# Side work between weight products: transposes emitted a step or two behind what makes their inputs

## The chip, the core and the metric

The kernel runs on one core of one Trainium2 chip. The metric is the device time of one launch in microseconds (us). The engines named below are PE (the matrix engine), DVE (the vector engine), ACT (the scalar engine), POOL (GpSimd) and SP (which starts most transfers). A transpose is a product on PE against the identity matrix; its result lands in PSUM and is copied out by DVE or ACT.

## What is computed

A step of a two-layer decoder trunk: 2048 new prompt tokens, and 8 sequences that each add 4 tokens to a state that is already there (the "sample"). Width 1024, fp32 throughout. Each layer, cut to what matters:

```
z = rms(x) @ w_in                       # aq, ak, av, ag, dqkv, dg, db, da
q = rope(rms(aq)); k = rope(rms(ak))    # 8 query heads, 2 key heads, 64 wide
att = sink_attend(q, k, av, window=128) * silu(ag)
q, k, v = split(silu(conv4(dqkv)))      # 4 heads, 128 wide
beta = sigmoid(db); g = -exp(a_log) * softplus(da + dt_bias)
dn = gated_delta(l2n(q), l2n(k), v, beta, g, state)
y = x + concat(att, rms(dn) * silu(dg)) @ w_out
```

The sample's rows go through the same layer with cached keys and values and a delta state of their own. The outputs are both rows, and the windows and states of each layer.

## The kernel before

The program goes through the two layers, and in each through four groups of 512 tokens. A group's input is held transposed, as a high and a low part in a rounded fp32 format, and a product with a block of weights takes three passes (high by high, high by low, low by high; `block`, L465). The weights come as a stream of pieces: SP fetches a piece, ACT rounds it (L248), POOL takes the rest (L249, `lo = raw - hi`). A group's blocks take some 68 pieces: keys, values and gates 0 to 3, the delta rule's keys 4 to 11, queries of the attention 12 to 19, the delta rule's queries 20 to 27 and values 28 to 35, two blocks of gates 36 to 51, and the output product 52 to 67.

All other work stands beside these products. It is written as generators, each with its `yield`s, and an object `Tasks` emits it between the pieces: `add(gen, n, s, e)` says that the generator has n steps, spread evenly over the pieces s to e, and `step()` runs, after each piece, as many as are due (the numbers stand in a table `W`). The order of emission is not yet the order on an engine: the framework's scheduler takes the emitted instructions, with their dependences, and sets for each engine its own order. On the engine itself instructions then run in that order, each waiting for its inputs.

The generators that the change touches:

- `k_task` normalises and rotates the group's keys (`head_norm_rope`, L370 to L384, on the tile `kall`), then transposes them, four transposes into one PSUM tile (L567), and copies them out as high and low (L571 to L573). It has one step, at piece 4.
- `q_task` does the same for the queries, in two halves of four heads each (`qh`), a step for each half, then for each of four tiles of tokens four transposes (L625) and copies (L629, L630).
- `att_task`, per tile of tokens: scores of a query tile with the keys (L647, L648, in two steps), exponentials, the division by their sum (L677, eight DVE instructions on the tile `Pt`), transposes of the softmax rows (L682), and the product with the values.
- `sample_att`: for the sample the softmax rows `Ps` are scaled (L1089) and transposed (L1094).
- `sample_head`: the delta rule of one head of the sample; its gated row (L426) is transposed in the last step (L1296). Within it also a product with the states (L1286).

Around them stand `gate_task` (the delta rule's gates: L397 to L410, copies into a tile `gx`, L585, then running sums as three products, L587, L597, L598) and `conv_tile`, the short convolution on DVE (L703 to L705) which empties the PSUM tiles of products. PSUM has four tiles for products (`mm`) and four for all else (`px`).

The step of the task list, which turns windows into emission:

```python
want = n if self.at >= e else n * (self.at - s) // (e - s)
while x[4] < want:
    next(gen, None)
    x[4] += 1
```

Of the kernel before, what the change touches and what calls it, by code (L numbers as in the profile page):

```python
# [24 lines left out]
TS = NB_S * LS  # L25
# [5 lines left out]
T = 512  # L31
# [6 lines left out]
# the blocks after the first one: (transposed, index), of k, k, aq, q, q, v, v, dg, ag, ag; where each lies in zs  # L38
# [4 lines left out]
# columns of the first constant array  # L43
C_ID, C_U, C_BAND = 0, 128, 256
C_END = 512
# windows of pieces in which the work beside the products with weights is emitted; see group()
W = dict(k1=4, pre0=13, pre1=19, q0=17, q1=31, inv0=20, inv1=41, invv=-3, att0=23, att1=46, qk0=36, qk1=38, sc0=44, sc1=52, sa0=-4, sa1=17, sp0=7, sp1=26, sh0=60, shd=8, shl=10, wla=4, wraw=4, xn0=2, xn1=8, sla=3, md0=53, md1=55, ma0=45)

# columns of the second one (sample): the rows are there three times
# [5 lines left out]
def _constants():  # L55
    i = np.arange(P)
    c = np.zeros((P, C_END), np.float32)
# [38 lines left out]
    # of kS and qS: row (4 b's, 32) -> tokens, k three times, q  # L96
# [17 lines left out]
class Tasks:  # L114
    """Work emitted between the pieces of the products with weights: each generator over a window of pieces."""
# [24 lines left out]
def hybrid_kernel(ctx, tc, a):  # L140
# [52 lines left out]
    def rsqrt(out, x):  # L193
        """x ** -0.5 of positive x: a guess from the exponent, three of Newton's steps"""
# [9 lines left out]
    def silu2(out, z, n, m):  # L204
        """2 silu(z), z in PSUM or SBUF"""
        th = f2([P, m], name="th")
        A.activation(th[:n], z, AF.Tanh, scale=0.5)  # L207
        V.scalar_tensor_tensor(out, th[:n], 1.0, z, op0=ALU.add, op1=ALU.mult)  # L208

    # keys of each group of heads, transposed, twice, as hi; then both groups' lo  # L210
# [25 lines left out]
    def fetch(first=False):  # L236
        """asks for the next pieces of the weights, as (hi, lo) of float32r, and whole"""
# [14 lines left out]
    def getw():  # L252
        """the next piece; later ones are under way"""
        fetch()
        return wready.pop(0)
# [43 lines left out]
    def x_norm(L, gi, out, first=False):  # L299
        """the group's input, transposed, [128, 2 k, T] each, and the factors of its norm on all partitions"""  # L300
# [31 lines left out]
    def x_scale(L, kh, x, out):  # L332
        """half of the normed input: [128, (hi lo), 4 k, T]"""
# [10 lines left out]
    def sx_stage(L, out):  # L344
        """the sample's normed input, transposed: [128, 8 k, TS]"""
# [18 lines left out]
    def head_norm_rope(x, n, gain, cos, sin):  # L364
        """RMS norm and rotation of x [n, a, b, 64] in place; cos, sin [n, a, 16]"""
# [20 lines left out]
    def gates(L, ba, n, c):  # L386
        """2 beta and log decay g of ba [n, c, 8] as [n, c, 4]"""
# [26 lines left out]
    def delta_out(po, rq, rq2, gate, on, n):  # L414
        """gated RMS norm of o = rq * po [n, m, 128]; the gain and a factor 0.5 are left out"""
# [12 lines left out]
    def qscale(ss, n, m):  # L428
        """the factors of q's norm from its sums of squares: r / sqrt(128), and that squared / 128"""
# [7 lines left out]
    def kscale(ss, b2, n, m):  # L437
        """beta / (2 |k|^2), and 0.5 sqrt of k's sums of squares"""
# [9 lines left out]
    def block(X, n, kpp, feat, consume, sg=None, every=1):  # L448
        """all tokens' columns of the next block of weights (or their transposes), k by k; X(k) gives the tokens'
        transposed rows [128, (hi lo), T]; sg, the sample's products, run ahead"""  # L450
# [23 lines left out]
    class SampleProducts:  # L474
        """the sample's products with the weights, a piece at a time, four tiles of the array at once: each k of the
        piece, parts of its columns; blocks are (columns, k per piece, consumer)"""
# [933 lines left out]
```

## Time and profile before

| | |
|---|---|
| median of 3 runs | 2594.18 us (2593.74 to 2595.14) |
| span of the profiled execution | 2594.2 us |
| PE busy | 2443.9 us, 94% of the span, 14580 instructions |
| DVE busy | 1844.2 us, 71% |
| ACT busy | 1183.7 us, 46% |
| POOL busy | 993.1 us, 38% |

The page lists busy time for each engine, then the span in slices, transfers, the chain of work that ended last, and the costliest groups of instructions. From the same execution a trace can be asked for the waits of an engine (who waited for whom, and how long), for a timeline of single instructions with the idle time before each, and for the busy time and the granted clock of PE in a stretch. Numbers such as L567 are lines of the kernel before. In the kernel with the change the same statement stands a few lines lower: L567 becomes L569, L585 and L587 become L587 and L589, L597 and L598 become L599 and L600, L625 and L630 become L628 and L633, L647 and L648 become L650 and L651, L682 becomes L687, L703 to L705 become L708 to L710, L1296 becomes L1303. L370 to L410 and L465 stay.

### The profile page before, as it was taken

The page shows a single profiled execution, that of the slowest core. Times are in us where ns is not written, and L with a number is a line of the kernel's source. Part 1 is how long each engine was busy: PE and PEld are TensorE (multiplying, and loading weights), DVE is VectorE, ACT ScalarE, POOL GpSimd, SP SyncE. Part 2 cuts the span into 40 slices and gives each one's busy share as a digit, 9 for nine tenths or more (in the row PEclk, how much of TensorE's full clock was granted, in tenths as well). Part 3 has the DMA queues.
Part 4 walks back from the last instruction along what each step waited for, and adds up shares of the span by engine and source line. Part 5 has one row for each costly group of instructions (what it writes and reads, how often), then busy time and mean ns, then how long its engine had stood idle before and what let it go on. Part 6 is the DMA issues. An engine that isn't in the chain of part 4 may idle for free. (4 is left out here: it accounts for less than half of the span.)

```text
span 2594.2 us, 43148 instructions
## 1 busy us (share of the span) xinstructions
PE 2443.9 (94%) x14580; PEld 1874.0 (72%) x14580; DVE 1844.2 (71%) x5509; ACT 1183.7 (46%) x3244; POOL 993.1 (38%) x1148
## 2 busy tenths in 40 slices
PE   6999999999999999999999999999998999999999
PEld 5766787668776677767876678776787667777677
DVE  6576777767788765776766757888577885767764
ACT  4444544445353444544534445444543444445442
POOL 2352353423424324353343523444243352344423
PEclk9988999889998999989999999999999999999999
DMA  3212342113432124211332113421233312232113
GB/s 125 83 58 60 112 144 80 49 48 106 143 102 67 52 74 147 92 49 54 108 121 81 54 50 129 135 83 42 84 119 115 101 55 84 83 125 82 52 46 110
DMA packets 185970, 227.30 MB, mean 88 GB/s; under 512 B 58524, under 2 KB 92932, under 8 KB 185684
## 3 DMA queue, kind: packets, MB, share of 16 engines
q1 hardware_dynamic: 185748, 224.54, 27.1%
q8 instruction: 115, 1.88, 0.3%
q14 instruction: 107, 0.88, 0.1%
HBM read 197.30 MB, written 30.19 MB: 88 GB/s over the span
## 5 line engine op out<-in xcount | busy, mean ns | idle before, releaser
L249 POOL TENSOR_TENSOR lo<-raw,hi 128x512 fp32r<-128x512 f32 (+1 forms) x576 | 748.4, 1304 | 1499.4 <-ACT hi L248 1469.4
L465 PE MATMUL mm<-xT,hi 128*128 128x512 f32 x2048 | 699.1, 412 | 4.7 <-ACT hi L248 3.6
L248 ACT CAST hi<-raw 128x512 fp32r<-128x512 f32 (+1 forms) x576 | 341.2, 595 | 604.6 <-PE mm L465 431.8
L465 PE MATMUL mm<-hi,xT 128*128 128x512 f32 (+1 forms) x1536 | 466.4, 377 | 4.7 <-DVE halo L705 2.9
L465 PEld LDWEIGHTS mm<-xT,hi 128*128 128x128 f32 x2048 | 399.6, 196 | 96.7 <-issue 7.7
L465 PE MATMUL mm<-xT,lo 128*128 128x512 f32 x1024 | 420.8, 411 | 0.4 <-POOL lo L249 0.3
L465 PEld LDWEIGHTS mm<-hi,xT 128*128 128x128 f32 x1536 | 280.5, 195 | 58.9 <-issue 14.3
L465 PE MATMUL mm<-lo,xT 128*128 128x512 f32 (+1 forms) x768 | 283.3, 369 | 0.0
L465 PEld LDWEIGHTS mm<-xT,lo 128*128 128x128 f32 x1024 | 201.7, 197 | 41.5 <-issue 1.9
L465 PE MATMUL mm<-mixA,hi 128*128 128x512 f32 x512 | 168.9, 398 | 0.0
L465 PE MATMUL mm<-mixD,hi 128*128 128x512 f32 x512 | 165.0, 394 | 0.0
L465 PEld LDWEIGHTS mm<-lo,xT 128*128 128x128 f32 x768 | 149.6, 195 | 18.4 <-issue 0.6
L652 DVE CUSTOM_DVE_ANT_0 Pt<-px,cst 128x256 f32<-128x256 f32 (+1 forms) x256 | 94.7, 413 | 95.3 <-PE px L648 94.5
L703 DVE SCALAR_TENSOR_TENSOR KQ<-mm,pc,KQ 128x511 f32<-128x511 f32 (+2 forms) x192 | 141.6, 738 | 23.9 <-ACT KQ L700 23.6
L666 ACT ACTIVATE Pt<-Pt,nm 128x256 f32<-128x256 f32 (+1 forms) x256 | 125.2, 491 | 8.2 <-DVE nm L658 8.2
L682 PE MATMUL px<-cst,Pt 128*128 128x128 f32 x496 | 92.9, 295 | 26.8 <-DVE Pt L677 24.2
L677 DVE TENSOR_SCALAR Pt<-Pt,rd 128x256 f32<-128x256 f32 (+1 forms) x256 | 116.4, 506 | 1.1
L772 POOL TENSOR_TENSOR Xh<-Xh,pr 128x126 f32<-128x126 f32 (+22 forms) x248 | 106.9, 431 | 18.1
L647 PE MATMUL px<-kT,q 128*128 128x256 f32 (+1 forms) x256 | 102.7, 401 | 11.4 <-ACT th L207 9.3
L465 PEld LDWEIGHTS mm<-mixD,hi 128*128 128x128 f32 x512 | 95.9, 188 | 23.1 <-issue 2.4
L770 POOL TENSOR_TENSOR pr<-At,Xh 128x126 f32<-128x126 f32 (+22 forms) x248 | 93.7, 378 | 48.0 <-DVE vT L208 16.1
L465 PEld LDWEIGHTS mm<-mixA,hi 128*128 128x128 f32 x512 | 96.4, 189 | 21.0 <-issue 2.0
(397 smaller groups left out, 4426.0 us busy)
## 6 DMA issues: line engine op xcount, KB each, us to landing
raw<-in_wf_dram SPq DMA_DIRECT2D x256, 256.0 KB
raw<-in_wt_dram SPq DMA_DIRECT2D x128, 256.0 KB
raw<-in_w_out_dram SPq DMA_DIRECT2D x128, 256.0 KB
raw<-in_w_dram SPq DMA_DIRECT2D x64, 132.0 KB
x<-in_x_prompt_dram SPq DMA_DIRECT2D x16, 512.0 KB
xr<-in_x_prompt_dram SPq DMA_DIRECT2D x32, 256.0 KB
y<-xr SPq DMA_DIRECT2D x32, 256.0 KB
x<-y SPq DMA_DIRECT2D x16, 512.0 KB
```

What stands on the lines that cost most here:

```text
L248: A.copy(hi, raw)
L249: G.tensor_sub(lo, raw, hi.bitcast(F32))
L465: PE.matmul(pss[u], lhs, rhs, start=(k == 0 and q == 0), stop=(k == 7 and q == 2))
L647: PE.matmul(sps[kv][:, jj, c0:], q, kT[:, kv, cols], start=True, stop=False)
L652: V.tensor_tensor_reduce(out=Pt[kv][:, j, c0:], in0=sps[kv][:, jj, c0:], in1=band[:, c0:], scale=1.0, scalar=NEG, op0=ALU.add, op1=ALU.max ...
L666: A.activation(Pt[kv][:, j, c0:], Pt[kv][:, j, c0:], AF.Exp, bias=nm[:, h:h + 1], scale=0.125, accum_out=den[:, h:h + 1])
L677: V.tensor_scalar(Pt[kv][:, j, c0:], Pt[kv][:, j, c0:], rd[:, h:h + 1], None, op0=ALU.mult)
L682: PE.transpose(pt[:, j, :], Pt[kv][:, j, kb * P:(kb + 1) * P], ident)
L703: V.scalar_tensor_tensor(dest[:, d:], ps[:, 0:T - d], w, dest[:, d:], op0=ALU.mult, op1=ALU.add)
L770: E.tensor_mul(pr, At[:, j, j + 1:].unsqueeze(2).to_broadcast([P, n, m]), Xh[:, j, 0:m].unsqueeze(1).to_broadcast([P, n, m]))
L772: E.tensor_sub(Xh[:, j + 1:, 0:m], Xh[:, j + 1:, 0:m], pr)
```

## The change

The generators get more `yield`s, and `add` gets the new numbers of steps. Comments and strings of documentation are gone, too. The instructions are the same, and each engine has as many of them as before.

```diff
-W = dict(k1=4, pre0=13, pre1=19, q0=17, q1=31, inv0=20, inv1=41, invv=-3, att0=23, att1=46, qk0=36, qk1=38, sc0=44, sc1=52, sa0=-4, sa1=17, sp0=7, sp1=26, sh0=60, shd=8, shl=10, wla=4, wraw=4, xn0=2, xn1=8, sla=3, md0=53, md1=55, ma0=45)
+W = dict(k1=4, pre0=13, pre1=19, q0=17, q1=29, inv0=20, inv1=41, invv=-3, att0=23, att1=46, qk0=36, qk1=38, sc0=44, sc1=52, sa0=-4, sa1=17, sp0=7, sp1=26, sh0=60, shd=8, shl=10, wla=4, wraw=4, xn0=2, xn1=8, sla=3, md0=53, md1=55, ma0=45)
...
         def k_task():
             head_norm_rope(kall, P, L.qkg[:, 0], cos, sin)
...
+            yield
+            yield
             pk = xt_([P, NT, P])
...
                 head_norm_rope(qhs[hb], P, None, cosq, sinq)
                 yield
+            yield
             g["q"] = []
...
                 V.reciprocal(rd, den)
                 yield
-                PT = []
                 for kv in range(2):
                     for j in range(4):
                         h = kv * 4 + j
                         V.tensor_scalar(Pt[kv][:, j, c0:], Pt[kv][:, j, c0:], rd[:, h:h + 1], None, op0=ALU.mult)
+                yield
+                PT = []
+                for kv in range(2):
                     ptt = f4([P, 2, T], name="PT")
...
-        add(k_task(), 1, 4, W["k1"])
+        add(k_task(), 3, 4, 8)
         add(gate_task(), 2, 4, 6)
...
-        add(q_task(qhs), 6, W["q0"], W["q1"])
+        add(q_task(qhs), 7, W["q0"], W["q1"])
         add(inv_task(), 38, W["inv0"], W["inv1"])
-        add(att_task(), 24, W["att0"], W["att1"])
+        add(att_task(), 28, W["att0"], W["att1"])
...
             V.tensor_scalar(Ps[:, b2], Ps[:, b2], den[:, b2:b2 + 1], None, op0=ALU.mult)
         yield
+        yield
         pt = xt_([P, 2, P])
...
         delta_out(o, L.srq[:n, hs], L.srq2[:n, hs], gate, o, n)
         yield
+        yield
         pt = xt_([P, n])
...
-                tk.add(sample_att(L), 10, at + W["sa0"], at + W["sa1"])
+                tk.add(sample_att(L), 11, at + W["sa0"], at + W["sa1"])
...
-                    tk.add(sample_head(L, h), 10, s, s + W["shl"])
+                    tk.add(sample_head(L, h), 11, s, s + W["shl"])
```

Of the hunks with a single new `yield` near the end, the one with `Ps` is in `sample_att`, the one with `delta_out` in `sample_head`. So the keys' norm is emitted at piece 6 instead of 4, and their transposes at piece 8. The windows of the softmax (23 to 46) and of the sample stay, with more steps in them.

What the engines' orders make of it is shown at three places. In these listings `mm<-xT,hi` is a product with weights (into a tile `mm`), `px` the other PSUM tiles; "x2" are instructions that follow each other with the same text.

PE, the keys of group 3 in layer 0. Before:

```order
L465 MATMUL mm<-xT,lo 128x512
L465 MATMUL mm<-xT,hi 128x512 x2
L567 MATMUL px<-cst,kall 128x128 x4
L587 MATMUL px<-cst,gx 128x128
L597 MATMUL px<-g,cst 128x16
L598 MATMUL px<-g,ones 128x16
```

With the change:

```order
L465 MATMUL mm<-xT,hi 128x512 x2
L465 MATMUL mm<-xT,lo 128x512
L589 MATMUL px<-cst,gx 128x128
L599 MATMUL px<-g,cst 128x16
L600 MATMUL px<-g,ones 128x16
L465 MATMUL mm<-xT,hi 128x512 x2
...
L465 MATMUL mm<-xT,hi 128x512
L569 MATMUL px<-cst,kall 128x128 x4
```

The four transposes of the keys stood ahead of the gates' products; now they stand behind them, with 19 further products with weights between, while the gates' products stand two products with weights earlier than the transposes did.

DVE at the same place (L376 to L384 are the keys' norm and rotation, L405 to L410 the gates, `gx` the tile that the gates' first product reads). Before:

```order
L376 TENSOR_TENSOR kall<-kall,qr 128x512
L405 SCALAR_TENSOR_TENSOR sp<-sp,sz_14046 128x16
L378 TENSOR_TENSOR kall<-kall,pb 128x512
L406 SCALAR_TENSOR_TENSOR sp<-sp,sz 128x16
L381 TENSOR_TENSOR rope<-kall,rot 128x128
L382 TENSOR_TENSOR rope<-kall,rot 128x8x8
L383 TENSOR_TENSOR rope<-kall,rot 128x8x8
L408 SCALAR_TENSOR_TENSOR sp<-sp,sx 128x16
L583 MEMSET gx 128x128
L384 TENSOR_TENSOR kall<-rope 128x8x16
L410 SCALAR_TENSOR_TENSOR g<-sp,ealog 128x16
L585 COPY gx<-g 128x16 x3
```

With the change:

```order
L406 SCALAR_TENSOR_TENSOR sp<-sp,sz 128x16
L202 SCALAR_TENSOR_TENSOR qr<-rs_t,qr 128x8
L408 SCALAR_TENSOR_TENSOR sp<-sp,sx 128x16
L376 TENSOR_TENSOR kall<-kall,qr 128x512
L410 SCALAR_TENSOR_TENSOR g<-sp,ealog 128x16
L378 TENSOR_TENSOR kall<-kall,pb 128x512
L587 COPY gx<-g 128x16 x3
L591 CAST G_14032<-px 128x128
L593 TENSOR_TENSOR rest<-px,G_14032 64x128
L381 TENSOR_TENSOR rope<-kall,rot 128x128
L594 CAST G_14032<-rest 64x128
L382 TENSOR_TENSOR rope<-kall,rot 128x8x8
```

The copies into `gx` stood behind the whole rotation; now they stand ahead of L381, but still behind L376 and L378.

PE, the queries and the first scores of group 0 in layer 0 (L625 or L628 transposes of queries, L647 or L650 the first scores). Before:

```order
L465 MATMUL mm<-xT,hi 128x512
L625 MATMUL px<-cst,qh 128x128 x2
L465 MATMUL mm<-xT,hi 128x512
L465 MATMUL mm<-xT,lo 128x512
...
L465 MATMUL mm<-xT,hi 128x512
L625 MATMUL px<-cst,qh 128x128 x2
L647 MATMUL px<-kT,q 128x128
L648 MATMUL px<-kT,q 128x128
```

With the change:

```order
L465 MATMUL mm<-xT,hi 128x512
L628 MATMUL px<-cst,qh 128x128 x2
L465 MATMUL mm<-xT,hi 128x512
L628 MATMUL px<-cst,qh 128x128 x2
L465 MATMUL mm<-xT,lo 128x512
L465 MATMUL mm<-xT,hi 128x512 x2
...
L465 MATMUL mm<-xT,hi 128x512
L650 MATMUL px<-kT,q 128x128
L651 MATMUL px<-kT,q 128x128
```

Between the two pairs of transposes of the first query tile lay 68 rows, nearly all of them products with weights; now there is one product, and the first scores follow behind some 11 more. On DVE there, with the change:

```order
L376 TENSOR_TENSOR qh<-qh,qr 128x1024
L202 SCALAR_TENSOR_TENSOR qr<-rs_t,qr 128x16
L381 TENSOR_TENSOR rope<-qh,cosq 128x256
L382 TENSOR_TENSOR rope<-qh,sinq 128x16x8
L383 TENSOR_TENSOR rope<-qh,sinq 128x16x8
L376 TENSOR_TENSOR qh<-qh,qr 128x1024
L384 TENSOR_TENSOR qh<-rope 128x16x16
L381 TENSOR_TENSOR rope<-qh,cosq 128x256
L382 TENSOR_TENSOR rope<-qh,sinq 128x16x8
L383 TENSOR_TENSOR rope<-qh,sinq 128x16x8
L765 MEMSET Xh 128x512
L384 TENSOR_TENSOR qh<-rope 128x16x16
```

The norm of the second half of the queries (the second L376 and L381 to L384) is now threaded with the first; before, it came behind four convolutions.

## Rows read from the trace of the kernel before

**Rows 1.** The page's head and first part: busy time, share, instructions.
```profile
span 2594.2 us, 43148 instructions
...
PE 2443.9 (94%) x14580; PEld 1874.0 (72%) x14580; DVE 1844.2 (71%) x5509; ACT 1183.7 (46%) x3244; POOL 993.1 (38%) x1148
```

**Rows 2.** Waits of PE: what waited <- for whom: total us, times, longest.
```profile
PE px L682 <- DVE Pt L677: 24.2, 40, 2.1
PE px L567 <- DVE kall L384: 18.4, 8, 3.0
...
PE px L625 <- DVE qh L384: 10.5, 7, 2.4
...
PE px L1296 <- DVE hw L426: 8.3, 4, 3.5
PE px L1094 <- DVE Ps L1089: 6.1, 2, 3.1
```

**Rows 3.** Windows: us, busy PE, PEld, DVE, ACT, POOL, granted clock, DMA share, GB/s.
```profile
149.00:171.00 22.00, 19.23 (x79) 12.46 (x80) 13.66 (x39) 9.96 (x30) 14.05 (x23) 0.53 0.16 53
1043.80:1048.10 4.30, 4.30 (x18) 3.62 (x19) 2.83 (x12) 2.39 (x6) 0.00 (x0) 0.61 0.29 92
```

**Rows 4.** PE's timeline, keys of group 3, layer 0: start, us, instruction, idle.
```profile
1040.39 0.39 PE L465 MATMUL mm<-xT,lo 128*128 128x512 f32 x1
1040.62 0.61 PE L465 MATMUL mm<-xT,hi 128*128 128x512 f32 x2
1043.77 0.66 PE L567 MATMUL px<-cst,kall 128*128 128x128 f32 x4 [2.54 <-DVE kall L384]
...
1044.96 0.78 PE L465 MATMUL mm<-xT,lo 128*128 128x512 f32 x1
```

**Rows 5.** Timeline of DVE at the same place.
```profile
1040.90 1.24 DVE L406 SCALAR_TENSOR_TENSOR sp<-sp,sz 128x16 f32<-128x16 f32 x1
...
1042.78 0.29 DVE L381 TENSOR_TENSOR rope<-kall,rot 128x128 f32<-128x128 f32 x1
...
1043.26 0.17 DVE L410 SCALAR_TENSOR_TENSOR g<-sp,ealog 128x16 f32<-128x16 f32 x1
1043.40 0.17 DVE L583 MEMSET gx<- 128x128 f32 x1
1043.49 0.23 DVE L384 TENSOR_TENSOR kall<-rope 128x128 f32<-128x128 f32 x1
1043.63 0.32 DVE L585 COPY gx<-g 128x16 f32<-128x16 f32 x3
```

**Rows 6.** Timeline of POOL (GpSimd) at the same place.
```profile
1040.43 1.69 POOL L249 TENSOR_TENSOR lo<-raw,hi 128x512 fp32r<-128x512 f32 x1 [1.41 <-ACT hi L248]
```

**Rows 7.** Timeline of PE, the keys of group 1, in layers 0 and 1.
```profile
382.00 0.66 PE L567 MATMUL px<-cst,kall 128*128 128x128 f32 x4 [1.74 <-DVE kall L384]
...
1666.19 0.66 PE L567 MATMUL px<-cst,kall 128*128 128x128 f32 x4 [2.14 <-DVE kall L384]
```

**Rows 8.** Timeline of DVE, queries and convolutions of group 0, layer 0.
```profile
112.90 1.22 DVE L372 TENSOR_REDUCE qss<-sq 128x16 f32<-128x1024 f32 x1 [2.60 <-ACT sq L370]
...
117.17 1.22 DVE L376 TENSOR_TENSOR qh<-qh,qr 128x1024 f32<-128x1024 f32 x1
...
119.71 0.36 DVE L384 TENSOR_TENSOR qh<-rope 128x256 f32<-128x256 f32 x1
...
122.70 0.75 DVE L703 SCALAR_TENSOR_TENSOR KQ<-mm,pc,KQ 128x511 f32<-128x511 f32 x1 [2.46 <-ACT KQ L700]
...
129.71 0.16 DVE L705 COPY halo<-mm 128x3 f32<-128x3 f32 x1
```

**Rows 9.** Timeline of PE in the same stretch, query transposes and first scores.
```profile
123.15 0.38 PE L625 MATMUL px<-cst,qh 128*128 128x128 f32 x2
...
149.04 0.33 PE L647 MATMUL px<-kT,q 128*128 128x128 f32 x1 [1.84 <-DVE q L630]
```

**Rows 10.** Timeline of PE, the sample's delta rule in layer 1.
```profile
2008.05 0.69 PE L1286 MATMUL px<-wbd,kd 96*128 96x512 f32 x2 [1.59 <-DVE wbd L1281]
```

## The prediction

> **What bounds the kernel now.** I read the page first: of the span, the matrix engine (PE) is busy 94%, every other engine at most 71% [rows 1]. So a microsecond is won only where PE stands still, where its clock is halved, or where its work shrinks; the change removes no work, it has the same instructions. Next I read the list of who PE waits for [rows 2]. The transposes that the change moves are five of its longest entries: softmax rows (L682) 24.2 us in 40 waits, keys (L567) 18.4 in 8, queries (L625) 10.5 in 7, sample rows (L1296) 8.3 in 4, sample softmax (L1094) 6.1 in 2: 67.5 us, 2.6% of the span. All end on VectorE (DVE). A wait also costs clock: behind the key wait of group 3 PE was granted 0.61 of full speed for 4.3 us, and 0.53 over the 22 us behind the first query tile of group 0 [rows 3], a mix of the two levels, 1.2 and 2.4 GHz. Then I read PE and DVE side by side at one such wait [rows 4, 5].
>
> The diff moves where steps are emitted. The scheduler then sets each engine's order, and there the same places hardly move. So each wait is costed by two counts from the order: how many products (PE, 0.23 us each, 1040.39 to 1040.62 in [rows 4]) now stand ahead of the waiting instruction, and how much DVE work stands ahead of what it waits for.
>
> **Keys, groups 0, 2 and 3 of both layers (six waits).** In the order the four transposes move behind about 19 more products, so they no longer wait. But the product that makes the running sums of the gates (L587; L589 in the change) stays, two products earlier than the transposes stood, and everything behind it waits with it. Before, its input was ready only a little after the keys: the copies (L585) start at 1043.63 and take 0.32 [rows 5]. In the change the scheduler still threads the norm through the gates' steps on DVE; ahead of the copies only the rotation (L381 to L383, 1042.78 to 1043.26), a memset (0.09) and L384 (0.14) are gone, 0.71 us. So the product can start at 1043.95 - 0.71 + 0.05 = 1043.29, against 1043.77 for the transposes before: 0.48 earlier, while PE arrives 2 x 0.23 = 0.46 earlier. The wait keeps its 2.5 us under another name. Gain 0.0 each; bounds -0.5 and +0.5 each, 3 us for six.
>
> PE holds everything behind a waiting product: products with the weights start only after the gates' ones, at 1044.96 [rows 4], though their weights were there. The Trainium skill says it as a rule (TensorE: Matmul & The Clock Gate, Part 3): matmuls start and end in program order, only weight loads are pulled ahead. The trace agrees; it speaks against the change, since taking one waiting instruction out of the row leaves the next one in front.
>
> One step on DVE (L406) takes 1.24 us at 1040.90 where its neighbours take 0.2, while GpSimd runs a subtraction of 1.69 us [rows 5, 6]; the same two overlap in the change unless weights come at another time, so a wait can come out 1 us longer or shorter. The Trainium skill (SBUF — State Buffer, SBUF: two separate sides) says that a DVE step with two SBUF inputs and a GpSimd step lock each other out of a shared port; the pair of rows agrees.
>
> **Keys, group 1 of both layers (two waits).** There the sample's gates run too, and the order on DVE puts the whole norm behind the copies. By mean durations of its lines that is about 5.4 us of DVE work less ahead of them, while PE arrives 12 products, 2.7 us, earlier. The copies end at most 1043.95 - 1043.49 = 0.46 behind the start of L384 [rows 5], so by about 382.4. So 382.0 - 2.7 is later than 382.4 - 5.4, and the waits of 1.74 and 2.14 [rows 7] go: -3.9. Bounds: 0 and -3.9 less one clock stretch of 1.7 each (4.3 x 0.39 from [rows 3]), -7.3.
>
> **Queries.** In seven of eight groups the first two transposes stand where they stood, and L384 with them: in group 3 it moves 0.95 later and then 1.14 earlier, while the second pair moves six products earlier. Net about 0.2 later per group, seven times: +1.2 (bounds -2 and +4). The third and fourth tiles come 4 to 12 us earlier, at places without a wait.
>
> **Softmax.** Of the longer waits several keep both counts to within three products; elsewhere the two counts shift together to within 1 us. 0, bounds -4 and +4; what would have to be hidden is 24.2 [rows 2].
>
> **Sample.** Ahead of the softmax transposes stand two products more, twice: -0.9. The transposes of rows keep their place for heads 0 and 3; in one head per layer three products fewer stand ahead: +1.4 for both. One wait of 1.59 in the second layer (L1286, [rows 10]) goes, as its DVE step moves 8.6 us earlier and PE only 4.8: -1.6.
>
> **Group 0 of layer 0.** Here the order does change. The emission step lets the scheduler put both norms of the queries together, ahead of the convolutions, and the first scores (L647; L650 in the change) move from behind some 100 products to 12 behind the queries. The first norm now has the reduction and the product of the second (1.22 each, [rows 8]) and small steps between: L384 ends not at 120.07 but near 123.8. PE arrives at 123.15 [rows 9] and waits 0.7; for the second pair another 1.4 (1.7 of DVE work against one product and two transposes). The scores then need the second half of q, and on DVE that stands behind two convolutions, 122.70 to 129.71, 7.0 us [rows 8], and takes 0.7 itself: 7.7 against 11 products, 2.5. A new wait of 5.2. In all 7.3 us of waits come. What goes: the 1.84 before the first scores [rows 9] and half of the 22.00 - 19.23 = 2.77 us that PE stands idle behind them [rows 3], together 3.3 (an estimate: the other half lies behind scores that still come as thinly). Clock: the old stretch, 19.2 us of busy PE at 0.53, costs 19.2 x 0.47 = 9.0; I take half of it as given back, since much of its work is still thin there, and 2.5 for a stretch behind the new wait. 7.3 - 3.3 - 4.5 + 2.5 = +2.0; bounds -5 (all given back) and +13 (none, and the new wait draws a stretch like the old one: 7.3 - 3.3 + 9).
>
> **The sum.** -3.9 + 1.2 + 0 - 0.9 + 1.4 - 1.6 + 2.0 = -1.8. The profiled execution's span is 2594.2 [rows 1], equal to the median, 2594.18, so no correction: 2592.4, said as 2592.
>
> **Rivals.** (1) *The waits do go.* If on the chip the gates' copies come before PE, for instance because DVE meets fewer GpSimd steps there, the six key waits go with their clock: 18.4 + 6 x 1.7 = 28.6, 2566; if all five kinds went, 67.5, 2527. For it: that is where the waits are. Against: both counts above, at each place. Chance 0.17. (2) *Slower: the first scores of group 0 wait and the clock goes with them.* Place: the 12 products behind the queries. Price at the upper bound, +13 instead of +2: -1.8 + 11 = +9, 2603. It decides the sign from the point where the clock there costs over 2 us more than I gave; for it speaks that a wait of 1.8 drew 22 us at 0.53 [rows 3, 9]; against, that dense products follow in the change. Chance 0.17. (3) *It does not do what it says:* the scheduler puts what is ready where it was ready, and shifts under 1 us even out: 2594. Chance 0.08.
>
> **How the numbers follow.** Forecast, another instruction takes over the waits: 2592, by itself 2585 to 2599, chance 0.58. About 0.2%, 5.2 us, is what a measurement tells from no change here: faster is under 2589.0, slower over 2599.4. Faster: 0.17 of rival 1 and a fifth of the forecast's 0.58, 0.29. Slower: most of rival 2 and a twentieth of the forecast, 0.17. Same: 0.54. The range for 8 in 10 leaves out most of rival 1 (0.13) and the far end of rival 2 (0.05): 2576 to 2604.
>
> **What would show it.** In the changed profile: L569 (keys) without idle time, and L589 with six waits of about 2 to 2.5 us, two near none; L628 and L1303 (sample rows) with waits as before; L687 (softmax) near 24 us in all; at 125 to 134 us a wait of about 5 before L650, and a granted clock above 0.53 from 149 to 171. The prediction is wrong if L589 does not wait, if the softmax waits fall by over 5 us, or if the first scores of group 0 find their queries ready.

## The result, and the profile after

The kernel with the change took 2617.0 us (median of 14 runs), the kernel before 2592.7 beside it; the ratio on record is 1.0085, with a 95% interval of 1.0062 to 1.0108 (the quotient of the two medians would be 1.0094). It became slower, and the time lies outside the range of the prediction (2576 to 2604). A second series of 6 runs gave 1.0078 (1.0047 to 1.0108). The profile of the change shown here is from the second series, since in the profiled execution of the first the clock was low over the whole span (0.816 of full speed, 2729.5 us); that execution is left out of the ratio and of the table below.

The page's head and first part, of the kernel with the change; PE stood at 2443.9 us of 2594.2 before [rows 1]:

```profile
span 2619.5 us, 43133 instructions
...
PE 2457.8 (94%) x14580; PEld 1891.1 (72%) x14580; DVE 1833.3 (70%) x5509; ACT 1181.6 (45%) x3244; POOL 977.9 (37%) x1148
```

So of 25.3 us PE is busy 13.9 longer with the same 14580 instructions, and idle 11.4 longer (2619.5 - 2457.8 = 161.7, against 150.3). The trace also tells at which clock PE ran: summed over the span, 281.4 us were at 1.2 GHz (below: at half clock), in 51 stretches, against 228.7 us in 36 before; the mean granted clock is 0.946 against 0.956.

The waits of PE with the change (what waited <- for whom: us in total, times, longest), to be held against [rows 2]:

```profile
PE px L687 <- DVE Pt L679: 16.4, 33, 0.9
...
PE px L589 <- DVE gx L587: 15.7, 6, 3.4
...
PE px L823 <- ACT Xc L817: 9.2, 7, 1.6
PE px L628 <- DVE qh L384: 8.3, 5, 3.6
PE px L1303 <- DVE hw L426: 6.8, 2, 3.4
PE px L650 <- DVE q L633: 6.7, 4, 2.6
...
PE px L589 <- DVE g L410: 4.1, 2, 2.1
...
PE px L1100 <- DVE Ps L1094: 3.6, 2, 1.8
...
PE px L569 <- DVE kall L384: 3.1, 2, 1.8
```

Two lines of the same list before, that [rows 2] leaves out (L818 is L823 with the change):

```profile
PE px L647 <- DVE q L630: 2.1, 2, 1.8
...
PE px L818 <- ACT Xc L812: 0.7, 4, 0.2
```

The softmax transposes (now L687) wait 16.4 instead of 24.2, the keys' (L569) 3.1 instead of 18.4, the queries' (L628) 8.3 instead of 10.5, the sample's rows (L1303) 6.8 instead of 8.3 and its softmax (L1100) 3.6 instead of 6.1: of the 67.5 us, 38.2 are left. But L589, the gates' product, now waits 15.7 + 4.1, a product of the inverse (L823) 9.2 where it waited 0.7 before, and the first scores (L650) 6.7 for their queries where they waited 2.1. The waits changed hands, and the clock fell.

**How clock and time hang together.** Each run lists its mean granted clock. Within one kernel the time follows it: over 253 runs in 17 series (of the kernel before 102; two of its 103 are alike in every figure and are counted once), the time changes by 1.99 us for each 0.001 of clock, and the spread of a kernel's runs falls from 7.0 us to 2.5 once that is taken out. So every kernel below is told twice: its ratio as measured, and its mean time brought to one clock, 0.957 (time + 1.99 x (clock - 0.957) / 0.001). The first is what counts; the second tells what came by waits and work, and the difference what came by the clock. The bringing to one clock is a fit, not a measurement. Intervals that hold 1 tell no change.

| kernel | median us | ratio, 95% interval | mean clock | us at 0.957 |
|---|---|---|---|---|
| before (102 runs) | 2595.9 | | 0.958 | 2595.6 |
| the whole change, first series | 2616.7 | 1.0085 (1.0062 to 1.0108) | 0.949 | 2599.3 |
| the whole change, again | 2615.3 | 1.0078 (1.0047 to 1.0108) | 0.948 | 2598.6 |
| keys alone | 2580.7 | 0.9948 (0.9920 to 0.9976) | 0.960 | 2587.0 |
| queries alone | 2598.4 | 1.0018 (0.9997 to 1.0039) | 0.960 | 2604.6 |
| softmax alone | 2588.4 | 0.9973 (0.9948 to 0.9998) | 0.957 | 2589.4 |
| sample alone | 2587.1 | 0.9982 (0.9959 to 1.0005) | 0.958 | 2592.9 |
| without the sample's part | 2623.6 | 1.0112 (1.0084 to 1.0140) | 0.946 | 2601.3 |
| without the queries' part | 2571.5 | 0.9921 (0.9893 to 0.9949) | 0.958 | 2576.4 |
| without the softmax part | 2593.3 | 1.0002 (0.9977 to 1.0028) | 0.959 | 2597.5 |
| window end alone of the queries' part | 2585.2 | 0.9972 (0.9947 to 0.9998) | 0.965 | 2600.2 |
| yield alone of the queries' part | 2583.0 | 0.9958 (0.9935 to 0.9980) | 0.960 | 2589.3 |
| no queries' part, gates' product later | 2559.9 | 0.9866 (0.9837 to 0.9894) | 0.960 | 2566.1 |
| whole, softmax from piece 24 | 2590.5 | 0.9984 (0.9966 to 1.0002) | 0.956 | 2586.9 |
| whole, softmax to piece 48 | 2556.8 | 0.9847 (0.9816 to 0.9879) | 0.968 | 2578.4 |
| whole, both edits | 2542.5 | 0.9792 (0.9759 to 0.9824) | 0.970 | 2568.7 |
| no queries' part, both edits | 2508.2 | 0.9662 (0.9631 to 0.9693) | 0.978 | 2550.6 |

### The profile page after: what moved, and what is told of

It reads as the page before. It is cut to its first block, busy times and chain, and to the rows that moved or that the text cites. A ratio compares the mean times of both kernels' runs of the same rounds, so it can differ in the third digit from the quotient of the medians.

```text
span 2727.7 us, 43133 instructions
## 1 busy us (share of the span) xinstructions
PE 2629.9 (96%) x14580; PEld 1953.4 (72%) x14580; DVE 1828.3 (67%) x5509; ACT 1184.6 (43%) x3244; POOL 973.5 (36%) x1148
## 5 line engine op out<-in xcount | busy, mean ns | idle before, releaser
L465 PE MATMUL mm<-xT,hi 128*128 128x512 f32 x2048 | 768.5, 446 | 7.5 <-ACT hi L248 4.7
L465 PEld LDWEIGHTS mm<-xT,hi 128*128 128x128 f32 x2048 | 417.1, 205 | 134.8 <-issue 10.6
L465 PE MATMUL mm<-hi,xT 128*128 128x512 f32 (+1 forms) x1536 | 497.4, 398 | 2.7 <-DVE halo L710 1.5
L465 PE MATMUL mm<-xT,lo 128*128 128x512 f32 x1024 | 453.9, 443 | 0.7 <-POOL lo L249 0.7
L465 PEld LDWEIGHTS mm<-hi,xT 128*128 128x128 f32 x1536 | 286.1, 199 | 66.3 <-issue 13.9
L465 PE MATMUL mm<-lo,xT 128*128 128x512 f32 (+1 forms) x768 | 300.5, 391 | 0.0
L465 PEld LDWEIGHTS mm<-xT,lo 128*128 128x128 f32 x1024 | 209.5, 205 | 59.1 <-issue 3.0
L465 PE MATMUL mm<-mixA,hi 128*128 128x512 f32 x512 | 183.0, 428 | 0.0
L465 PE MATMUL mm<-mixD,hi 128*128 128x512 f32 x512 | 178.6, 422 | 0.0
L465 PEld LDWEIGHTS mm<-lo,xT 128*128 128x128 f32 x768 | 153.0, 199 | 26.4 <-issue 0.6
L465 PEld LDWEIGHTS mm<-mixD,hi 128*128 128x128 f32 x512 | 98.2, 192 | 33.0 <-issue 3.1
L465 PEld LDWEIGHTS mm<-mixA,hi 128*128 128x128 f32 x512 | 98.9, 193 | 30.0 <-issue 2.1
L650 PE MATMUL px<-kT,q 128*128 128x256 f32 (+1 forms) x256 | 103.1, 404 | 12.8 <-ACT th L207 4.7
L775 POOL TENSOR_TENSOR pr<-At,Xh 128x126 f32<-128x126 f32 (+22 forms) x248 | 92.5, 373 | 59.2 <-DVE vT L208 14.9
L465 PE MATMUL mm<-mixA,lo 128*128 128x512 f32 x256 | 108.2, 423 | 0.0
L465 PE MATMUL mm<-mixD,lo 128*128 128x512 f32 x256 | 107.4, 419 | 0.0
L651 PE MATMUL px<-kT,q 64*128 64x256 f32 (+1 forms) x256 | 106.4, 419 | 0.0
```

Source lines behind the costliest of these rows:

```text
L465: PE.matmul(pss[u], lhs, rhs, start=(k == 0 and q == 0), stop=(k == 7 and q == 2))
L650: PE.matmul(sps[kv][:, jj, c0:], q, kT[:, kv, cols], start=True, stop=False)
L651: PE.matmul(sps[kv][:, jj, c0:], q[r], kT[r, 2, cols], start=False, stop=True)
L775: E.tensor_mul(pr, At[:, j, j + 1:].unsqueeze(2).to_broadcast([P, n, m]), Xh[:, j, 0:m].unsqueeze(1).to_broadcast([P, n, m]))
```

## Experiments

### The parts alone

The whole change again, and each part of it by itself in the kernel before: of the diff shown above, the hunks of `k_task` (keys), of `q_task` with `q1` (queries), of `att_task` (softmax), and of `sample_att` and `sample_head` (sample).

> The whole change once more, for a profile beside the kernel before. Theory A (clock): the 24 us that its median lies above the kernel before are PE at half clock for longer stretches, not waits: the mean granted clock is lower than the 0.956 of before by about 0.008 (0.948), PE's busy time is about 20 us more, its idle time about equal or less. Theory B (waits): the granted clock is 0.956 as before, and PE's idle time is about 24 us more. Both expect 2610 to 2622 us, ratio about 1.008.

> The keys' part alone (two yields more in k_task, three steps over pieces 4 to 8). The prediction's count: L589 takes over six of eight waits, -3.9 us, so 2588 to 2592, ratio 0.998 to 1.000. Theory A if it lies here: the transposes and the gates' products are two interruptions of PE instead of one, each of them with a stretch at half clock; over eight groups some 10 to 20 us, ratio 1.004 to 1.008, with the granted clock lower than 0.956.

> The queries' part alone (one yield more in q_task, seven steps over pieces 17 to 29). The prediction's count: +1.2 and +2.0 for group 0 of layer 0, so 2595 to 2600, ratio 1.000 to 1.002, up to 1.005 if the first scores of group 0 draw a stretch at half clock. If the loss lies here the ratio is 1.006 or more, and the waits of the query transposes or of the first scores in the trace grow.

> The softmax part alone (the scaling of the rows in a step of its own, 28 steps over pieces 23 to 46). The prediction's count: 0, bounds -4 and +4, ratio 0.998 to 1.002. If the loss lies here, the ratio is 1.005 or more: then steps that are spread otherwise over the pieces break PE's row of products more often, and the granted clock falls between 23 and 46 pieces of a group.

> The sample's part alone (one yield more in sample_att and sample_head, 11 steps each). The three other parts alone came out at 0.9948 (keys), 1.0018 (queries) and 0.9973 (softmax), together -0.6%, while the whole change came out at 1.0078. Theory A (the parts add up): the sample's part costs the rest, 1.4%, ratio 1.014. Theory B (the parts disturb each other): it costs little by itself, ratio 0.998 to 1.003. The prediction's own count for it is -0.9 + 1.4 - 1.6 us, ratio 0.9996.

The keys alone win 0.5%, the softmax 0.3%; the sample's gain of 0.2% and the queries' loss of 0.2% have intervals that hold 1. The keys and the softmax are a little better than their expectations (0.998 to 1.000 and 0.998 to 1.002). Added up that is a gain of 0.8%; the whole change loses 0.8%. Of theories A and B of the first expectation both hold in part: the clock is lower by 0.010 and PE's idle time larger by 11.4 us. No single part lowers the clock: 0.957 to 0.960 in all four.

### One part left out at a time

> The whole change without the sample's part. Theory A (adding up): the sum of the three parts, ratio 0.994. Theory B with the queries' and the softmax part as the pair that collides: ratio 1.006 to 1.010, as the whole change; in the trace the wait of 2.6 us before the first scores of group 0 and the waits of 1.4 us before L823 stand as in the whole change, with a granted clock of 0.946 to 0.950.

> The whole change without the queries' part. Theory A (adding up): -0.5 - 0.3 + 1.4 = +0.6%, ratio 1.006. Theory B (queries and softmax collide): 0.990 to 0.995, clock 0.955 or more, since the first scores of group 0 stand again far behind their transposes and each softmax step again meets the pieces that it met in the softmax part alone.

> The whole change without the softmax part. Theory A (adding up): -0.5 + 0.2 + 1.4 = +1.1%, ratio 1.011. Theory B (queries and softmax collide): 0.995 to 0.999, the keys' gain and the queries' small loss; the waits of 1.4 us before the inverse's product (L818 of the kernel before) are gone from the trace.

Theory B (the parts disturb each other, queries and softmax as the pair) is borne out: with both the clock is 0.946 to 0.949, with one of the two left out 0.958 and 0.959. (Without the softmax part the ratio is 1.0002, just above the 0.995 to 0.999 that was expected; without the sample's part 1.0112, just above 1.006 to 1.010.) At one clock keys, softmax and sample add up: -8.6 - 6.2 - 2.7 = -17.5, against -19.2 found without the queries' part. With queries and softmax together (without the sample's part) the sum would be -8.6 + 9.0 - 6.2 = -5.8, and +5.7 was found, besides a clock lower by 0.012, 24 us. So the pair costs some 35 us, by the fit, that neither part costs by itself. The keys' part was there in each of these kernels; the pair without it was not run.

### Which half of the queries' part

The first kernel is the whole change without the new yield in `q_task`, with six steps to piece 29:

```diff
-            yield
             g["q"] = []
...
-        add(q_task(qhs), 7, W["q0"], W["q1"])
+        add(q_task(qhs), 6, W["q0"], W["q1"])
```

The second keeps the yield and ends the window at 31 as before; the softmax then has to start a piece later (`att0=24` instead of 23). The third is the whole change with `att0=24` alone.

> The whole change, but in the queries' part only the window's end (17 to 29), without the yield: six steps, the tiles of queries at pieces 23, 25, 27 and 29. Theory W (window): the loss comes from the query tiles that are emitted closer together, into the same pieces as the softmax's first steps; then the ratio stays at 1.006 to 1.012 and the granted clock at 0.944 to 0.950. Theory Y (yield): it comes from the yield, which puts both norms together and the first scores close behind the transposes; then it falls to 0.990 to 0.997, as without the queries' part (0.9921).

> The whole change, but the queries' window ends at 31 as before, with the yield (seven steps, tiles at pieces 25, 27, 29 and 31); since the first tile then comes a piece later, the softmax's window starts at 24 instead of 23. Theory W: 0.990 to 0.997 with a clock of 0.953 or more, since the tiles are spread as before. Theory Y: 1.006 to 1.012. In the trace: whether the first scores of group 0 still wait 2.6 us close behind the transposes, and whether stretches at half clock follow the scores of group 3 in stage v, where the whole change has 6.8 us in both layers and the softmax part alone none.

> The whole change with the softmax's window starting at piece 24 instead of 23; the queries' part stays whole. The two runs with one half of the queries' part (0.9972 and 0.9958) leave open whether it was the half left out, or in the second of them the softmax's start, that took the loss away. Theory P (place): what counts is which softmax steps fall beside which query tiles; a shift by one piece takes the loss away: 0.993 to 0.998, clock 0.957 to 0.963, and in its order the small products of PE stand in fewer separate groups than in the whole change. Theory Y (the queries' part as a whole, wherever the softmax stands): 1.006 to 1.012, clock 0.945 to 0.950.

Neither half is enough by itself: in the first two kernels the loss is gone (0.9972 and 0.9958), and so it is when both halves stay and the softmax starts one piece later (0.9984). Since the second kernel has that later start too, it does not tell what its window's end does alone. Theories W and Y fall both, each by one of the first two kernels; theory P (place) stands, with a ratio and a clock (0.956) just outside what it expected: what counts is which softmax steps come beside which query tiles. The window's end alone is a case of its own: at one clock it is the slowest but two (2600.2), with 165.0 us of idle time of PE, yet its clock is one of the higher ones (0.965). More waits do not mean a lower clock.

### Where the clock falls

With the whole change the blocks of the delta rule's queries and values and the first block of gates (pieces 20 to 43, over all groups) hold 218.7 us at half clock, before 169.5; the other blocks hold 62.7 and 59.2. A place that shows how it falls is the values' block of group 3 in layer 0. PE with the whole change, from the products with values (L694) over the scores (L650, L651) to the products with weights (L465); start, us, instruction:

```profile
1136.99 2.06 PE L694 MATMUL px<-PT,vt 128*64 128x512 f32 x8
1138.98 0.39 PE L650 MATMUL px<-kT,q 128*128 128x256 f32 x1
...
1141.48 0.50 PE L465 MATMUL mm<-xT,hi 128*128 128x512 f32 x1
...
1144.16 0.58 PE L651 MATMUL px<-kT,q 64*128 64x256 f32 x1
1144.67 0.79 PE L465 MATMUL mm<-xT,lo 128*128 128x512 f32 x1
```

And its windows there (us, busy time of PE, PEld, DVE, ACT, POOL, granted clock, DMA share, GB/s):

```profile
1136.90:1144.70 7.80, 7.80 (x27) 3.89 (x26) 5.36 (x17) 1.44 (x3) 3.58 (x9) 0.92 0.11 36
1143.50:1150.40 6.90, 6.90 (x17) 5.09 (x17) 4.20 (x16) 0.62 (x1) 1.28 (x1) 0.51 0.12 40
```

The same place with the softmax part alone, where L691 are the products with values, L647 and L648 the scores, L625 transposes of queries:

```profile
1139.98 1.07 PE L691 MATMUL px<-PT,vt 128*64 128x512 f32 x2
1140.99 0.38 PE L647 MATMUL px<-kT,q 128*128 128x256 f32 x1
...
1142.24 1.07 PE L691 MATMUL px<-PT,vt 128*64 128x512 f32 x2
1143.24 0.38 PE L647 MATMUL px<-kT,q 128*128 128x256 f32 x1
...
1144.49 0.50 PE L465 MATMUL mm<-xT,lo 128*128 128x512 f32 x1
1144.83 0.60 PE L625 MATMUL px<-cst,qh 128*128 128x128 f32 x4
1145.18 0.71 PE L465 MATMUL mm<-xT,hi 128*128 128x512 f32 x2
...
1147.81 0.38 PE L648 MATMUL px<-kT,q 64*128 64x256 f32 x1
1148.12 0.50 PE L465 MATMUL mm<-xT,lo 128*128 128x512 f32 x1
```

```profile
1140.00:1148.20 8.20, 8.20 (x29) 4.29 (x28) 5.20 (x17) 2.23 (x4) 4.71 (x9) 1.00 0.09 32
```

In both PE is never idle there (7.80 of 7.80 and 8.20 of 8.20 us busy). With the whole change eight products with values and sixteen with keys stand in a row with a single product with weights between, and at 1143.5 the clock falls, 0.51 over the next 6.9 us. With the softmax part alone a query tile's transposes and three products with weights stand between, and products with values and scores alternate; the clock stays at 1.00. The same holds in layer 1, and in the run without the sample's part (6.8 us at half clock in each of these four blocks, none in the four of the kernel with the softmax part alone and of the kernel without the queries' part). With the queries' part the query tile is transposed ahead of the scores instead of among them; that this is what lets the scores move together is read from the order, not tested by itself. The kernel before loses as much in this very block, behind six products with values and ten scores, so it is no place where the two kernels differ; the first block of gates of group 3, shown further below, is (13.7 us at half clock in either layer, 3.4 before):

```profile
1150.50:1157.40 6.90, 6.90 (x16) 4.63 (x16) 4.13 (x16) 0.87 (x2) 0.00 (x0) 0.51 0.08 28
```

The orders bear it out as far as the ends go. Rows of 24 scores and products with values, with at most one other instruction of PE between two of them: 4 in the kernel before, 2 with the keys alone, 6 with the softmax alone, 8 with the queries alone, 10 with the whole change and without the sample's part, where the clock is lowest. In between the count does not rank the kernels: the window's end alone has 8 such rows and a clock of 0.965. Rows of at least 12 scores alone (L650, L651) are 16 before, 27 with the whole change and without the sample's part, and 4 with the later end of the next section; in between they do not rank the kernels either (22 with the queries alone, at a clock of 0.960).

Counted over the span: of 51 stretches at half clock with the whole change 22 (116 us) have no wait over 0.3 us in the 7 us ahead of them (a stretch of time taken for this count); before, 15 of 36 (85 us). What stands there instead are scores: each of the 22, and each of the 15, has ten or more of them in those 7 us, and 8 of the 22 and 7 of the 15 have no product with values. The Trainium skill (TensorE: Matmul & The Clock Gate, Part 1, on oscillation) describes the fall of the clock as what follows idle gaps of PE. Behind some waits the traces agree (1.84 and 2.54 us, [rows 3, 4, 9]); the 22 stretches here have none, so the measurement decides: the clock also falls behind stretches in which PE hardly stood still.

In none of the 16 traces does the clock fall behind a row of products with values that has no scores beside it, unless PE waited. Such a row stands in the kernel of the next section, behind transposes (L687) and ahead of products of the delta rule (L905, L913), and the clock over these 12 us is 1.00:

```profile
1863.25 2.85 PE L694 MATMUL px<-PT,vt 128*64 128x512 f32 x8
```

```profile
1861.00:1873.00 12.00, 11.62 (x67) 8.35 (x65) 8.57 (x25) 5.35 (x16) 2.71 (x2) 1.00 0.66 209
```

### Thinner steps

The whole change with `att1=48` instead of 46: the 28 softmax steps now share 25 pieces instead of 23, so fewer pieces carry two.

```diff
-W = dict(k1=4, pre0=13, pre1=19, q0=17, q1=29, inv0=20, inv1=41, invv=-3, att0=23, att1=46, qk0=36, qk1=38, sc0=44, sc1=52, sa0=-4, sa1=17, sp0=7, sp1=26, sh0=60, shd=8, shl=10, wla=4, wraw=4, xn0=2, xn1=8, sla=3, md0=53, md1=55, ma0=45)
+W = dict(k1=4, pre0=13, pre1=19, q0=17, q1=29, inv0=20, inv1=41, invv=-3, att0=23, att1=48, qk0=36, qk1=38, sc0=44, sc1=52, sa0=-4, sa1=17, sp0=7, sp1=26, sh0=60, shd=8, shl=10, wla=4, wraw=4, xn0=2, xn1=8, sla=3, md0=53, md1=55, ma0=45)
```

> The whole change with the softmax's window ending at piece 48 instead of 46, so that fewer of its 28 steps fall on one piece with another. Theory C (crowding): the clock falls where small products (transposes, scores, products with values) stand on PE in a row with hardly a product with weights between; in this order such places are fewer, so the clock rises to 0.955 or more and the ratio falls to 0.990 to 0.998. Theory S (splitting): the clock falls once for each separate group of small products that is long enough, and the whole change has more groups (51 stretches at half clock against 37); thinner spreading leaves as many groups or makes more, so the clock stays at 0.944 to 0.952 and the ratio at 1.004 to 1.014.

The clock rises to 0.968 and the ratio falls to 0.9847, the way that theory C (crowding) said and beyond its 0.990 to 0.998. Theory S, more groups, more falls, is out: 31 stretches are left, 8 of them (34 us) without a wait ahead. In the order no row of 20 or more scores and products with values is left. The first block of gates of group 3 (layer 0) shows it: windows of before, of the whole change and of this kernel (columns as above):

```profile
1167.80:1226.70 58.90, 57.56 (x458) 40.75 (x457) 41.29 (x121) 25.62 (x76) 17.75 (x31) 0.97 0.19 51
```

```profile
1160.60:1223.80 63.20, 61.04 (x459) 43.81 (x458) 38.41 (x124) 25.42 (x80) 17.57 (x29) 0.89 0.17 47
```

```profile
1150.50:1206.30 55.80, 54.51 (x458) 39.78 (x456) 37.46 (x121) 29.67 (x94) 15.85 (x24) 1.00 0.20 55
```

The clock there is 0.97, 0.89 and 1.00, the length 58.9, 63.2 and 55.8 us. PE in the whole change: sixteen scores in a row from 1176.06, then the delta rule's transposes (L852); the clock falls at 1181.0.

```profile
1176.06 0.36 PE L650 MATMUL px<-kT,q 128*128 128x256 f32 x1
...
1180.74 0.38 PE L651 MATMUL px<-kT,q 64*128 64x256 f32 x1
1181.05 1.11 PE L852 MATMUL px<-cst,KQ 128*128 128x128 f32 x4
```

And with the later end: eight scores, transposes and products of the delta rule (L852, L857), and eight scores again, 3.4 us later.

```profile
1167.18 0.38 PE L650 MATMUL px<-kT,q 128*128 128x256 f32 x1
...
1169.37 0.38 PE L651 MATMUL px<-kT,q 64*128 64x256 f32 x1
1169.68 0.66 PE L852 MATMUL px<-cst,KQ 128*128 128x128 f32 x4
...
1171.51 1.06 PE L857 MATMUL px<-KQ 128*128 128x128 f32 x8
...
1173.06 0.38 PE L650 MATMUL px<-kT,q 128*128 128x256 f32 x1 [0.26 <-ACT junk L854]
...
1175.25 0.38 PE L651 MATMUL px<-kT,q 64*128 64x256 f32 x1
```

Two steps of scores that stood together are parted. PE's row of small instructions is no shorter here, only mixed otherwise, so it is not small products as such. What the falls without a wait have in common are the scores; what in the scores lets the clock fall (every second one, L651, uses 64 of 128 rows) is not told by these runs.

### The keys' wait, handed on

The prediction's step on the keys said that the wait passes to L589 since PE holds everything behind a waiting product. In `gate_task` of the kernel without the queries' part:

```diff
             for i in (0, 2, 3):
                 V.tensor_copy(gx[:, i, 0:NC], gf)
+            yield
+            yield
+            yield
             pt = xt_([P, P])
...
-        add(gate_task(), 2, 4, 6)
+        add(gate_task(), 5, 4, 9)
```

> The change without the queries' part (0.9921), and in gate_task three yields between the copies into gx and the product that reads them (L589), five steps over pieces 4 to 9: the product then stands right behind the keys' transposes, some 27 products with weights later. If the prediction's step on the keys is right (the wait was handed on from the keys to the next product in PE's order), the eight waits of L589, 15.5 + 4.3 us in the keys' part alone, go, and no other instruction takes them, since what stands there now are products with weights that are ready: idle time of PE 18 to 20 us less, and with the half clock behind these waits (3.4 to 6.8 us each) 25 to 35 us in all, ratio 0.979 to 0.984. If the next instruction waits again, 0.990 to 0.994.

With the change the wait of group 3 (layer 0) stands before L589; [rows 4] shows it before L567, 2.54 us long:

```profile
1036.56 0.39 PE L465 MATMUL mm<-xT,lo 128*128 128x512 f32 x1
1039.64 0.49 PE L589 MATMUL px<-cst,gx 128*128 128x128 f32 x2 [2.69 <-DVE gx L587]
...
1040.33 0.72 PE L465 MATMUL mm<-xT,hi 128*128 128x512 f32 x2
```

With the product moved (L569 the keys' transposes, L592 the gates' product) nothing waits there:

```profile
1014.96 0.66 PE L569 MATMUL px<-cst,kall 128*128 128x128 f32 x4
1015.45 0.39 PE L592 MATMUL px<-cst,gx 128*128 128x128 f32 x2
1015.60 0.48 PE L465 MATMUL mm<-xT,hi 128*128 128x512 f32 x1
```

Idle time of PE in the blocks of pieces 4 to 11 (the delta rule's keys) falls from 27.6 to 14.4 us, and the ratio from 0.9921 to 0.9866, less than expected (0.979 to 0.984): in group 1 of both layers the keys' transposes wait again, 3.4 and 2.7 us. So the mechanism holds in six groups of eight, and gives some 13 us of waits there (8.3 over the span) and little clock (0.958 to 0.960).

### Both edits together

> The whole change with both edits that helped: the gates' product three steps later (as in r3_gates_later) and the softmax's window to piece 48 (as in r4_att_end). If the two are independent: 0.9847 less the 0.0055 that the gates' step gave there, 0.979. If they disturb each other as the queries' and the softmax part do: 0.985 to 0.995.

> The same without the queries' part. If the softmax's later end helps only where it undoes the collision with the queries, it gives nothing here: 0.986, as r3_gates_later. If thinner steps help by themselves (theory C, crowding): 0.972 to 0.979, with a clock of 0.965 or more.

With the queries' part the ratio is 0.9792, as two independent edits would give. Without it 0.9662: 2508.2 us, the fastest kernel here, and past what either theory expected. Its page's head and first part:

```profile
span 2510.7 us, 43119 instructions
...
PE 2385.6 (95%) x14580; PEld 1842.7 (73%) x14580; DVE 1815.9 (72%) x5509; ACT 1184.8 (47%) x3244; POOL 989.5 (39%) x1148
```

Against [rows 1] PE is busy 58.2 us less with the same 14580 instructions, and idle 25.3 us less (125.0 against 150.3). At half clock are 116.0 us in 20 stretches instead of 228.7 in 36. Thinner softmax steps help without the queries' part too: from 0.9866 to 0.9662, with the later end as the only difference. The later end was not tried in the kernel before.

## Right and wrong, step by step

- **Keys.** Right: L589 waits 15.7 us in six groups, 2.6 each (predicted 2 to 2.5 each), and L569 is free there. Wrong in group 1: L589 waits 4.1 in two and L569 3.1 in two, where -3.9 us were counted: 3.3 more than before instead. PE's idle time in the blocks of pieces 4 to 11 is 26.5 us after 26.4. That the keys alone win 0.5% was not counted: their idle time fell by 3.2 us, most of it in the block of the delta rule's queries (27.2 to 23.3), where the step moves nothing that the prediction looked at; the rest of its 8.6 us at one clock these rows do not explain.
- **Queries.** L628 waits 2.2 us less for the norm than before, counted was +1.2: a miss just outside its bound of -2. Its waits for two other steps of DVE (L633, L769) grew by as much.
- **Softmax.** Counted at 0, bounds -4 and +4; the transposes wait 7.8 us less, which the prediction named as a sign of its being wrong, and the inverse's product L823 8.5 more. In sum near nothing, but by two moves, of which the second was not seen: the step was read at the softmax's waits alone, not at what takes their place on PE. The inverse's wait comes with the softmax part alone too (8.7), so it is not what makes the pair lose.
- **Sample.** Softmax rows -2.5 (counted -0.9), rows -1.5 (counted +1.4), L1286's wait gone as counted. Its part alone gave 0.9982.
- **Group 0 of layer 0.** The mechanism came as described: the first scores stand close behind their transposes and wait for the second half of q, which DVE copies behind two convolutions. The wait is 2.65 us, not 5.2, as the two convolutions take 4.9 us there, not 7.0, and the waits of 0.7 and 1.4 before the transposes do not come:

```profile
125.95 0.39 PE L465 MATMUL mm<-xT,hi 128*128 128x512 f32 x1
128.99 0.33 PE L650 MATMUL px<-kT,q 128*128 128x128 f32 x1 [2.65 <-DVE q L633]
```

 The clock there was priced in the right direction, at half its size both ways. The windows of the new scores' stretch (0.99 before) and of the old one (0.53 before, [rows 3]) are

```profile
129.00:151.00 22.00, 21.89 (x94) 15.87 (x95) 6.49 (x20) 5.96 (x10) 11.01 (x15) 0.77 0.28 88
149.00:171.00 22.00, 18.67 (x105) 14.00 (x104) 11.25 (x37) 9.29 (x29) 8.68 (x14) 0.92 0.15 50
```

 By these windows 8.6 us come back (22 x 0.39, counted 4.5) and 4.8 are drawn (22 x 0.22, counted 2.5). But two waits that the prediction did not have follow, one for weights and one before scores, and 13.7 us at half clock from 180.9 with them:

```profile
163.00 0.73 PE L465 MATMUL mm<-xT,hi 128*128 128x512 f32 x2 [2.62 <-ACT hi L248]
...
181.97 0.58 PE L650 MATMUL px<-kT,q 128*128 128x256 f32 x1 [3.95 <-ACT m L698]
```

 The group's three blocks of pieces 20 to 43 took 137.2 us after 130.8: +6.4, predicted +2 within -5 and +13. Their time at half clock did not fall but rose, from 29.9 to 34.1 us, and PE's idle time rose from 7.6 to 13.4. This is the place of rival 2, and half of its price. (The prediction's 3.3 of waits that go there adds up to 3.2, which changes nothing.)
- **The sum.** The step that failed is the price of the clock. In the forecast it was set at one place (group 0, +2.5 - 4.5) and as something that follows a wait; for seven groups it was taken as nothing, since no wait grew. In fact the time at half clock grew by 52.7 us over the span, 49 of them in the blocks where queries, softmax and inverse stand beside the products, and 31 of them behind no wait but behind scores that stand closer together. The mean clock was 0.949 instead of 0.958: 17 of the 21 us in the table (8.4 x 1.99, by the fit); waits and work came out at +3 to +4 against -1.8. That these are only 5 to 6 us off is in part luck: the terms of the waits miss both ways, by +7.2 (keys of group 1), -3.4 (queries) and -4.5 (sample). The trace of before held the hint: 15 of its 36 stretches at half clock follow no wait. The prediction looked only at those behind one.
- **Rivals.** None of the three happened as told: rival 1's waits did not go, rival 2 has the sign and a part of its place, rival 3 is out.

## What to carry to other kernels

When PE is busy 94%, price an edit of the order twice: by waits, and by what it puts side by side on PE, since the clock can halve behind a long row of certain products (here scores) although nothing waits. Spread such steps so that no two of them meet (here the clock rose from 0.948 to 0.968 by that), and try the parts of a change in pairs, not only alone: two that alone gave 1.0018 and 0.9973 made the whole 0.8% slower. A wait that is handed to the next instruction in PE's order goes only when that one is moved too.

## What the runs showed of the hardware

- The granted clock of the same program differs from run to run (0.948 to 0.968 in 102 runs of the kernel before), and its time with it, 2613.5 to 2575.2 us: 1.99 us for 0.001. A difference under about 0.5% between two kernels here needs the clock beside it.
- The clock fell to 1.2 GHz behind stretches in which PE was busy throughout (7.80 of 7.80 us) with scores and products with values, and one kernel had more waits (165.0 us idle) at a higher clock (0.965) than another with 161.7 at 0.948.
- All 22 falls without a wait in the trace of the whole change, and all 15 before, stand behind ten or more scores. Eight products with values in a row (2.85 us), between transposes and products of the delta rule, were not followed by a fall (1.00 over 12 us). What exactly in the scores decides is open.
